# Score, bias and last-expert products on all 128 rows of the array, and the experts' gate cap moved behind its function

## Chip, cores and metric

The kernel runs on one core of one Trainium2 chip. The metric is the device time of one execution in microseconds (us). A profiled execution gives the trace that is quoted below; times of unprofiled runs give the median.

## What is computed

One layer of a decoder on x of 1024 tokens x 1024 channels, in float32. The reference, cut to the parts that the change touches:

```python
s = jnp.einsum('bdhnqc,bdhnkc->bdhnqk', qs, kk)      # 8 heads of 64 channels, causal, three dilated patterns
...
def expert_block(args):                               # top 4 of 32 experts per token
    tok, e = args
    xb = h_pad[tok]
    g = jnp.minimum(xb @ w_gate[e] + b_gate[e], SWIGLU_LIMIT)
    u = jnp.clip(xb @ w_up[e] + b_up[e], -SWIGLU_LIMIT, SWIGLU_LIMIT)
    act = (u + 1.0) * (g * jax.nn.sigmoid(SWIGLU_ALPHA * g))
    return act @ w_down[e] + b_down[e]
```

SWIGLU_LIMIT is 7, SWIGLU_ALPHA 1.702. Ahead of the experts stand an input projection, a gated unit along chunks of 128 tokens, the attention, an output projection with a layer norm, and the router; behind them a last layer norm.

## The kernel before

**Precision.** TensorE (PE) multiplies float32 operands that were split in two: a rounded part in the format fp32r (`h`) and the rest (`l`). A product of two splits takes three matmuls, high x high, low x high and high x low (`mm3`, L122 to L125).

**Front (to about 575 us).** Tokens and weights are loaded and split, and four head groups g = 0 to 3 go through the steps that the string `FRONT` names: V (values and the gated unit's input), K and Q (keys and queries), A (attention), U and S (the gated unit). The program is written in that order, but a scheduler orders the instructions of each engine, so projections of the next group stand between the attention's steps. Then the output projection (`mix`), the layer norm and the router follow for eight tiles of 128 tokens.

The attention of one group handles two heads, 64 channels each. `queries` puts each head's rounded queries on rows 0 to 63 and once more on rows 64 to 127 (`qh[h]`); the rest of both heads shares one tile `ql`, each on its own 64 rows. `keys` puts the rounded keys of a head on its own 64 rows of `ks[h]` and their rest on the other 64. So one product over 128 rows gives qh x (kh + kl), and a second one over the head's own 64 rows adds ql x kh:

```python
TE.matmul(ps[:, :w], qh[h][:, t], ks[h][:, b:b + w], start=True, stop=False)    # L371
TE.matmul(ps[:, :w], ql[c, t], ks[h][c, b:b + w], start=False, stop=True)       # L372, c: 64 rows
```

The width w is at least 256. DVE adds the mask table and takes the minimum (L373), ACT exponentiates (L376), DVE scales (L378), PE transposes (L384), ACT or DVE copies (L388, L386), and PE multiplies by the values (L393, 64 columns of the array). Working tiles named `t2` (three buffers) serve the two tanh chains and the gated unit.

**Experts (about 600 to 1970 us).** 32 experts are sorted by load into slots; `CAPS` gives each slot's room: 16 wide ones (136 to 256 tokens), 15 narrow ones of 128 and a last one of 64. A wide expert and a narrow one alternate. For each expert 12 weight pieces of 1 MB come in through SP's queue (`load`, L772) into five `raw` buffers, ACT rounds a piece to fp32r (L119), DVE makes the rest in bf16 (L120), and up to four split pieces are held. In a wide expert the weights stand still in the array (`weights_still`, L821) and tokens stream; biases are added per partition from a table `bias` (L858). In a narrow one the tokens stand still (`tokens_still`, L812) and weights stream 512 columns wide; the biases come in as a first product of a one-hot tile `oh` with the bias rows `bhl`, both on 64 rows (L835). The last expert, of 64 tokens, puts high and low tokens side by side in 128 columns, and its low products on 64 columns.

The activation stands in `gu_chain` (narrow, L695) and `gate_up_wide` (L843 on): DVE caps the gate at 7 (L698, L862), ACT applies the function (L699, L863), DVE clips up to -7..7 (L700, L867), and one DVE instruction computes (up + 1) x gate (L701, L868). The instructions on SP are kept in the order in which they are written; those of the other engines are ordered by the scheduler. The loop for left-over tokens behind the experts runs zero times or more, by data.

Of the kernel before, what the change touches and what calls it, by code (L numbers as in the profile page):

```python
# [10 lines left out]
FT = mybir.dt.float32  # L11
# [11 lines left out]
D = 1024  # L23
P = 128
# [9 lines left out]
LIMIT = 7.0  # L34
GELU_C = math.sqrt(2.0 / math.pi)
# [41 lines left out]
def layer(tc, i, out):  # L77
# [22 lines left out]
    perm = cp.tile([64, E], FT, name="perm")  # L100
# [211 lines left out]
    def sgu(g):  # L312
        vn, u, (ws, bs) = vn_of.pop(g), u_of.pop(g), ws_of.pop(g)
        at = big("t4", 3)
        for half in range(2):
            ps = bank("mm", (P, 4, P))
            for n in range(4):
                for h in range(2):
                    TE.matmul(ps[h * 64:h * 64 + 64, n], vn[:, half * 4 + n, h * 64:h * 64 + 64],
                              ws[:, h, :], start=True, stop=True)  # L320
            t = A.tile([P, 512], FT, name="t2", bufs=3)
            V.tensor_tensor(t.rearrange("p (n c) -> p n c", c=P), ps,
                            bs.to_broadcast([P, 4, P]), op=OP.add)
            d = slice(half * 512, half * 512 + 512)
            V.scalar_tensor_tensor(at[:, d], u[:, d], 0.5, t, op0=OP.mult, op1=OP.mult)
        store(0, g, at)

    q_of, k_of = {}, {}

    def queries(g, proj):  # L330
        qh = [big(f"qh{h}", 1, FR) for h in range(2)]
        ql = big("ql", 1, FR)
# [9 lines left out]
        q_of[g] = qh, ql  # L342

    def keys(g, proj):
        ks = [big(f"ks{h}", 1, FR) for h in range(2)]
        for half in range(2):
            ps = proj(half)
            s = slice(half * 512, half * 512 + 512)
            for h in range(2):
# [4 lines left out]
        k_of[g] = ks  # L354

    def attend(g):
        (qh, ql), ks, va = q_of[g], k_of[g], va_of[g]
        bt = big("t4", 3)
        for qt in range(NT):
            n = (qt + 1) * P  # L360
            pts = []
            for h in range(2):
                c = slice(h * 64, h * 64 + 64)
# [3 lines left out]
                for b in range(0, n, 512):  # L367
# [4 lines left out]
                    TE.matmul(ps[:, :w], ql[c, t], ks[h][c, b:b + w], start=False, stop=True)  # L372
# [88 lines left out]
    zero = A.tile([P, 512], FT, name="t2", bufs=3)  # L461
# [47 lines left out]
    bd = A.tile([3 * E, D], FR, name="ql")  # L509
# [31 lines left out]
    def rank():  # L541
# [10 lines left out]
        V.tensor_scalar(perm, ie[:64], kc[:, 1:2], None, op0=OP.is_equal)  # L552
# [4 lines left out]
    def logits(t, x, sums):  # L557
# [17 lines left out]
        else:  # L575
            V.tensor_scalar(mu[:, 1:2], mu[:, 0:1], 1.0 / 32, None, op0=OP.mult)
            sq = A.tile([P, 2], FT, name="sq", bufs=2)
            for q in range(2):
                junk = A.tile([P, 512], FT, name="t2", bufs=3)
# [115 lines left out]
    def gu_chain(pool, gp, up, n, tag, dst, inside=False):  # L695
        g = gp if inside else pool.tile([P, 512], FT, name=tag, bufs=3)
        u = up if inside else pool.tile([P, 512], FT, name=tag, bufs=3)
        V.tensor_scalar(g[:n], gp, LIMIT, None, op0=OP.min)  # L698
        S.activation(g[:n], g[:n], AF.Gelu_apprx_sigmoid)  # L699
        V.tensor_scalar(u[:n], up, -LIMIT, LIMIT, op0=OP.max, op1=OP.min)  # L700
        V.scalar_tensor_tensor(dst[:n], u[:n], 1.0, g[:n], op0=OP.add, op1=OP.mult)  # L701

    with (tc.tile_pool(name="c", bufs=1, reuse_waits="tile") as C,
          tc.tile_pool(name="cpsum", bufs=1, space=PSUM, reuse_waits="tile") as CP):
        left = C.tile([64, P], FT, name="left")
        V.memset(left, 0.0)
        V.memset(left[:, 0:64], 1.0)
        onesr = C.tile([64, P], FT, name="onesr")
# [15 lines left out]
        def fetch(r):  # L724
# [30 lines left out]
        def prepare(b):  # L755
# [3 lines left out]
            b.Xb = C.tile([P, KT, n], BF, name="xb" + size)  # L759
# [5 lines left out]
            if not b.wide:  # L765
                b.oh = C.tile([64, P], FR, name="oh", bufs=2)
# [36 lines left out]
        def tokens_still(p, n, x, xb, h, l, kq, first):  # L803
# [41 lines left out]
        def gate_up_wide(b, half, between):  # L845

            n, v = b.n, []
            for m in range(2):
# [12 lines left out]
                if m == 0:  # L861
                    V.tensor_scalar(t, t, LIMIT, None, op0=OP.min)  # L862
# [4 lines left out]
            V.tensor_scalar(u, u, -LIMIT, LIMIT, op0=OP.max, op1=OP.min)  # L867
            V.scalar_tensor_tensor(u, u, 1.0, g, op0=OP.add, op1=OP.mult)  # L868
# [5 lines left out]
        def room(b):  # L874
# [4 lines left out]
            b.Ab = C.tile([P, KT, b.n], BF, name="ab" + size)  # L879

        def turn(b, half):
            if not b.wide:
                c, n = slice(half * 4, half * 4 + 4), b.n
                turned(b.A[:, c, 0:n], b.A[:, c, n:2 * n], b.Ab[:, c],
# [42 lines left out]
        bhl = C.tile([64, 2, D], FR, name="bhl")  # L927

        def narrow_biases():
            for n in range(2):  # L930
# [3 lines left out]
                S.activation(bhl[:, n], br, AF.Copy)  # L934
# [34 lines left out]
    with tc.For_i(0, more, 1) as j:  # L969
        with tc.tile_pool(name="o", bufs=1) as O, tc.tile_pool(name="op", bufs=1, space=PSUM) as OPS:  # L970
# [37 lines left out]
            for half in range(2):  # L1008
                d = slice(half * 512, half * 512 + 512)
                v = []  # L1010
                for m in range(2):
                    ps = times(xs, e, [half * 4 + m, half * 4 + 2 + m])
                    t = O.tile([P, 512], FT, name="gu", bufs=2)
                    V.tensor_tensor(t, ps, bias[:, m, d], op=OP.add)
# [96 lines left out]
```

## Time and profile before

| what | value |
| --- | --- |
| median of 3 runs | 2012.61 us (2011.72 to 2015.56) |
| the profiled execution | 2018.92 us |
| its span, first to last instruction | 2017.1 us |
| mean granted clock of TensorE | 0.973 of full speed |
| DMA, mean over the span | 246 GB/s |

How to read it: busy times of engines overlap, so they don't add up to the span. PE is TensorE's matmuls, PEld its weight loads, DVE the vector engine, ACT the scalar engine, POOL GpSimd, SP the queue that issues most transfers. A row names the line, the engine, the operation and the tiles it writes and reads. For PE the row also has the part of the array that is used: 128\*128 is the full array, 64\*128 half of its rows, 128\*64 half of its columns. The clock has two levels, 1.2 and 2.4 GHz, and the mean of a stretch says how long each was granted.

### The profile page before, as it was taken

How to read it: one execution, taken by the hardware profiler on the slowest of the kernel's cores; microseconds unless marked ns; L12 is line 12 of the kernel's file. 1: busy time of each engine (PE TensorE's matmuls, PEld its weight loads, DVE VectorE, ACT ScalarE, POOL GpSimd, SP SyncE). 2: the span in 40 equal slices, each digit the busy share in tenths (PEclk: the TensorE clock that was granted, in tenths of full speed). 3: DMA queues.
4: the chain of work that ended last, by engine and by line, in shares of the span. 5: the costliest groups of instructions: out<-in, count | busy, mean ns of one | idle time of the engine just before them, and what ended most of it. 6: DMA issues, size and time to landing. Idle time of an engine off the chain costs nothing.

```text
span 2017.1 us, 32818 instructions
## 1 busy us (share of the span) xinstructions
PE 1915.5 (95%) x12423; PEld 1560.2 (77%) x12484; DVE 1582.4 (78%) x2233; ACT 1332.9 (66%) x1761; POOL 306.4 (15%) x197
## 2 busy tenths in 40 slices
PE   7999999999949999999999999999999999999991
PEld 6787686678837888788888888888888888888861
DVE  4644745577759798788888888888988988988895
ACT  4443434563337787687778778778877887887873
POOL 2112110042320112021101102011111110101110
PEclk9999999989969999999999999999999999999996
DMA  5111010162258898799889889988989989998874
GB/s 188 45 47 45 24 39 11 37 202 80 90 207 298 277 366 296 277 322 367 296 285 360 302 314 324 359 322 300 364 308 316 363 306 335 329 344 335 307 271 174
DMA packets 92657, 495.94 MB, mean 246 GB/s; under 512 B 20264, under 2 KB 20824, under 8 KB 43344
## 3 DMA queue, kind: packets, MB, share of 16 engines
q1 hardware_dynamic: 76128, 442.49, 59.6%
q0 software_dynamic: 14064, 42.92, 8.7%
q10 hardware_dynamic: 2304, 8.39, 1.1%
q8 instruction: 100, 1.64, 0.3%
q14 instruction: 61, 0.50, 0.1%
HBM read 457.04 MB, written 36.72 MB: 245 GB/s over the span
## 4 chain that ended last, share of the span: by engine, by line
PE 61%; DVE 4%; DMA 3%; ACT 2%; issue 1%; POOL 0%; SPq 0%; POOLq 0%; ACTq 0%; DVEq 0%
PE b L821 32%; PE b L812 24%; PE b L751 2%; DVE wl L120 2%; ACT wh L119 2%; PE b L920 1%; PE b L835 1%; DMA raw<-in_w_moe 1%; DMA ys<-o,tg 1%; DVE y L1056 1%; DVE y L1055 0%; DMA table<-pay,dst 0%; POOL table L626 0%; DMA y<-ys 0%; DMA xg<-hs,tg 0%
## 5 line engine op out<-in xcount | busy, mean ns | idle before, releaser
L120 DVE TENSOR_TENSOR wl<-raw,wh 128x2048 bf16<-128x2048 f32 (+1 forms) x385 | 877.0, 2283 | 135.9 <-ACT wh L119 130.7
L119 ACT ACTIVATE wh<-raw 128x2048 fp32r<-128x2048 f32 (+1 forms) x394 | 742.9, 1894 | 149.9 <-PE b L812 41.1
L821 PE MATMUL b<-xw,wh 128*128 128x272 f32 (+12 forms) x2048 | 353.4, 326 | 0.0
L821 PEld LDWEIGHTS b<-xw,wh 128*128 128x128 f32 x2048 | 319.8, 189 | 12.4
L812 PE MATMUL b<-wh,xt 128*128 128x512 f32 x992 | 271.0, 414 | 0.0
L821 PEld LDWEIGHTS <-wl 128*128 128x128 bf16 x3072 | 225.7, 98 | 15.1 <-issue 5.6
L812 PEld LDWEIGHTS b<-wh,xt 128*128 128x128 f32 x992 | 181.3, 188 | 59.7 <-issue 15.7
L742 POOL DMA_INDIRECT xg<-hs,tg x48 | 73.7, 1536 | 838.4 <-PE b L751 391.2
L821 PE MATMUL b<-aw,wh 128*128 128x272 f32 (+12 forms) x1024 | 174.3, 325 | 0.0
L923 POOL DMA_INDIRECT ys<-o,tg x48 | 113.5, 2364 | 376.8 <-ACT o L921 156.4
L821 PE MATMUL b<-xbw,wl 128*128 128x136 bf16 (+12 forms) x2048 | 165.9, 239 | 0.0
L821 PEld LDWEIGHTS b<-aw,wh 128*128 128x128 f32 x1024 | 159.6, 188 | 6.1
L856 ACT ACTIVATE sb<-b 128x136 f32<-128x136 f32 (+12 forms) x256 | 78.3, 317 | 90.3 <-PE b L821 85.4
L812 PE MATMUL b<-wh,at 128*128 128x512 f32 x496 | 137.0, 417 | 0.0
L812 PE MATMUL b<-wl,xbt 128*128 128x512 bf16 (+1 forms) x467 | 116.0, 380 | 2.7
L812 PEld LDWEIGHTS b<-wh,at 128*128 128x128 f32 x496 | 92.5, 189 | 25.4 <-issue 2.0
L858 DVE SCALAR_TENSOR_TENSOR tw<-b,bias,sb 128x136 f32<-128x136 f32 (+12 forms) x256 | 91.6, 393 | 14.5 <-ACT sb L856 13.7
L812 PEld LDWEIGHTS <-xbt 128*128 128x128 bf16 (+1 forms) x512 | 45.3, 99 | 62.8 <-issue 17.8
L821 PE MATMUL b<-abw,wl 128*128 128x136 bf16 (+12 forms) x1024 | 83.0, 239 | 0.0
L908 ACT ACTIVATE sb<-b 128x136 f32<-128x136 f32 (+12 forms) x128 | 38.8, 314 | 60.1 <-PE b L821 51.0
L388 ACT ACTIVATE pt<-tp 128x512 f32<-128x512 f32 (+3 forms) x80 | 38.0, 498 | 59.2 <-PE tp L384 58.9
L123 PE MATMUL mm<-xh,wh 128*128 128x512 f32 x160 | 69.5, 434 | 6.5 <-DVE ks L353 6.5
(357 smaller groups left out, 2930.2 us busy)
## 6 DMA issues: line engine op xcount, KB each, us to landing
raw<-in_w_moe SPq DMA_DIRECT2D x384, 1024.0 KB, 7.0
raw<-in_w_in SPq DMA_DIRECT2D x18, 512.0 KB, 3.7
raw<-in_w_out SPq DMA_DIRECT2D x8, 512.0 KB, 3.7
t<-in_x SPq DMA_DIRECT2D x8, 512.0 KB, 3.4
hs<-pt ACTq DMA_DIRECT2D x8, 512.0 KB, 5.1
ys<-pr ACTq DMA_DIRECT2D x8, 512.0 KB, 2.6
y<-ys SPq DMA_DIRECT2D x8, 512.0 KB, 6.6
out<-y SPq DMA_DIRECT2D x8, 512.0 KB, 2.6
```

The source lines that it names most:

```text
L119: S.activation(hi, src, AF.Copy)
L120: by.tensor_tensor(lo, src, hi.bitcast(FT), op=OP.subtract)
L123: TE.matmul(o, ah, bh, start=start, stop=False)
L388: S.activation(pt[:, b:e], tp[:, :e - b], AF.Copy)
L742: k.got = G.indirect_dma_start(out=k.x[:k.n], out_offset=None, in_=hs, in_offset=bass.IndirectOffsetOnAxis(ap=k.idx, axis=0))
L751: TE.transpose(tp[:, j], src(j), ident[:n, :n])
L812: TE.matmul(o, a, b, start=first and q == 0, stop=kq == 1 and q == len(every) - 1)
L821: TE.matmul(o, a, b, start=kq == 0 and j == 0, stop=kq == 1 and j == 3)
L856: S.activation(x2[:, :n], p[f][:, n:2 * n], AF.Copy)
L858: V.scalar_tensor_tensor(t[:, f * n:f * n + n], p[f][:, :n], b.bias[:, c:c + 1], x2[:, :n], op0=OP.add, op1=OP.add)
L908: S.activation(x2[:, :n], p[:, n:2 * n], AF.Copy)
L923: G.indirect_dma_start(out=ys, out_offset=bass.IndirectOffsetOnAxis(ap=k.idx, axis=0), in_=k.o[:k.n], in_offset=None, compute_op=OP.add)
```

## The change

1. **Scores.** Each head gets a `ql[h]` of its own, in bf16, zero on the other head's 64 rows; the keys are also kept as one bf16 tile `kb` (a DVE copy out of PSUM, 8 of 128 x 512). The second score product then runs over all 128 rows, in bf16, and is only as wide as needed.
2. **Bias products.** `oh` and `bhl` get 128 rows, the upper 64 of them zero.
3. **Last expert.** `Xb` and `Ab` are padded with zeros from 64 to 128 columns, so that its low products use the full array.
4. **Gate.** The cap at 7 moves behind the function: min(f(x), TOP) with TOP = f(7), inside the final DVE instruction. ACT reads the gate's sum directly. The "+ 1" of up goes into its bias (for wide experts one DVE instruction of 128 x 8 per expert behind the bias transfer, for narrow ones once), and the clip becomes -6..8.
5. `t2` has two buffers instead of three; the tile `bd` takes the room of `ssq1` instead of `ql`.

The diff, cut to what is spoken of:

```diff
+TOP = LIMIT / (1.0 + math.exp(-1.702 * LIMIT))
...
-        s = A.tile(shape, FT, name="t2", bufs=3)
+        s = A.tile(shape, FT, name="t2", bufs=2)
...
+    ql = [big(f"ql{h}", 1, BF) for h in range(2)]
+    for h in range(2):
+        G.memset(ql[h][64 - h * 64:128 - h * 64], 0.0)
...
-                V.scalar_tensor_tensor(ql[c, s], ps[c], -0.125, qh[h][c, s].bitcast(FT),
+                V.scalar_tensor_tensor(ql[h][c, s], ps[c], -0.125, qh[h][c, s].bitcast(FT),
...
+        kb = big("kb", 1, BF)
         for half in range(2):
             ps = proj(half)
             s = slice(half * 512, half * 512 + 512)
+            V.tensor_copy(kb[:, s], ps)
...
                     TE.matmul(ps[:, :w], qh[h][:, t], ks[h][:, b:b + w], start=True, stop=False)
-                    TE.matmul(ps[:, :w], ql[c, t], ks[h][c, b:b + w], start=False, stop=True)
+                    TE.matmul(ps[:, :e - b], ql[h][:, t], kb[:, b:e], start=False, stop=True)
...
-        V.tensor_scalar(g[:n], gp, LIMIT, None, op0=OP.min)
-        S.activation(g[:n], g[:n], AF.Gelu_apprx_sigmoid)
-        V.tensor_scalar(u[:n], up, -LIMIT, LIMIT, op0=OP.max, op1=OP.min)
-        V.scalar_tensor_tensor(dst[:n], u[:n], 1.0, g[:n], op0=OP.add, op1=OP.mult)
+        S.activation(g[:n], gp, AF.Gelu_apprx_sigmoid)
+        V.tensor_scalar(u[:n], up, 1.0 - LIMIT, 1.0 + LIMIT, op0=OP.max, op1=OP.min)
+        V.scalar_tensor_tensor(dst[:n], g[:n], TOP, u[:n], op0=OP.min, op1=OP.mult)
...
+                V.tensor_scalar(b.bias[:, 8:], b.bias[:, 8:], 1.0, None, op0=OP.add)
...
-            b.Xb = C.tile([P, KT, n], BF, name="xb" + size)
+            b.Xb = C.tile([P, KT, max(n, P)], BF, name="xb" + size)
+            if n <= 64:
+                G.memset(b.Xb[:, :, n:], 0.0)
...
-                b.oh = C.tile([64, P], FR, name="oh", bufs=2)
+                b.oh = C.tile([P, P], FR, name="oh", bufs=2)
...
-            rows = [slice(0, n), slice(n, 2 * n)] if n > 64 else [slice(0, 64 + n)]
-            high = [(p[:n] if n > 64 else p[:64 + n], x[:, k, r], h[:, k % 4]) for k in ks for r in rows]
-            low = [(p[:n], xb[:, k], l[:, k % 4]) for k in ks]
+            rows = [slice(0, P), slice(P, 2 * n)][:n // 64]
+            high = [(p, x[:, k, r], h[:, k % 4]) for k in ks for r in rows]
+            low = [(p, xb[:, k], l[:, k % 4]) for k in ks]
...
-                    V.tensor_scalar(t, t, LIMIT, None, op0=OP.min)
...
-            V.tensor_scalar(u, u, -LIMIT, LIMIT, op0=OP.max, op1=OP.min)
-            V.scalar_tensor_tensor(u, u, 1.0, g, op0=OP.add, op1=OP.mult)
+            V.tensor_scalar(u, u, 1.0 - LIMIT, 1.0 + LIMIT, op0=OP.max, op1=OP.min)
+            V.scalar_tensor_tensor(u, g, TOP, u, op0=OP.min, op1=OP.mult)
...
-            b.Ab = C.tile([P, KT, b.n], BF, name="ab" + size)
+            b.Ab = C.tile([P, KT, max(b.n, P)], BF, name="ab" + size)
+            if b.n <= 64:
+                G.memset(b.Ab[:, :, b.n:], 0.0)
...
-        bhl = C.tile([64, 2, D], FR, name="bhl")
+        bhl = C.tile([P, 2, D], FR, name="bhl")
+        G.memset(bhl[64:].bitcast(FT), 0.0)
...
-                S.activation(bhl[:, n], br, AF.Copy)
+                if n:
+                    V.tensor_scalar(br, br, 1.0, None, op0=OP.add)
+                S.activation(bhl[:64, n], br, AF.Copy)
```

**How the order moves.** The rows below are those of the built programs, in the order in which an engine takes them; a row stands for equal instructions that follow each other. First PE near the end of the last group's attention, before (L371 and L372 the two score products, L384 transposes, L393 the product with the values, L123 to L125 a projection of the gated unit):

```order
L393 MATMUL po<-pt,va 64x128 x11
L371 MATMUL s<-ks_3225,qh_3125 128x512
L372 MATMUL s<-ks_3225,ql 128x512
L371 MATMUL s<-ks_3225,qh_3125 128x512
L372 MATMUL s<-ks_3225,ql 128x512
L371 MATMUL s<-ks_3226,qh_3126 128x512
L372 MATMUL s<-ks_3226,ql 128x512
L125 MATMUL mm<-xh_130,wl 128x512
```

and of the change (line numbers are higher by five: L376 and L377 are the score products, L389 transposes, L398 the values):

```order
L126 MATMUL mm<-xh_142,wl 128x512
L398 MATMUL po<-pt,va 64x128 x11
L376 MATMUL s<-ks_3234,qh_3135 128x512
L377 LDWEIGHTS ql_174
L377 MATMUL s<-kb,ql_174 128x512
L376 MATMUL s<-ks_3235,qh_3136 128x512
L389 MATMUL tp<-ident,pr 128x128 x7
L377 LDWEIGHTS ql_175
L377 MATMUL s<-kb,ql_175 128x512
L124 MATMUL mm<-xh_148,wh 128x512
L125 MATMUL mm<-xl_149,wh 128x512
```

The second score product now has a weight load in a row of its own and reads `kb` and one head's `ql`. Two of the projection's products that stood between the scores stand elsewhere; the scheduler has ordered this whole stage anew.

DVE, in the second half of a narrow expert, before (L120 splits weights and tokens, L698 caps the gate, L700 clips up, L701 multiplies):

```order
L120 TENSOR_TENSOR wl<-raw,wh 128x2048
L698 TENSOR_SCALAR t<-b 128x512
L120 TENSOR_TENSOR wl<-raw,wh 128x2048
L767 TENSOR_SCALAR oh<-onesr,perm 64x128
L120 TENSOR_TENSOR at<-b,at 128x4x128
L120 TENSOR_TENSOR wl<-raw,wh 128x2048
L700 TENSOR_SCALAR t<-b 128x512
L120 TENSOR_TENSOR wl<-raw,wh 128x2048
L701 SCALAR_TENSOR_TENSOR act<-t 128x512
L120 TENSOR_TENSOR wl<-raw,wh 128x2048
```

and of the change (L121, L706 and L707 are the split, the clip and the product):

```order
L121 TENSOR_TENSOR wl<-raw,wh 128x2048 x2
L776 TENSOR_SCALAR oh<-onesr,perm 128x128
L121 TENSOR_TENSOR at<-b,at 128x4x128
L121 TENSOR_TENSOR wl<-raw,wh 128x2048
L706 TENSOR_SCALAR t<-b 128x512
L707 SCALAR_TENSOR_TENSOR act<-t 128x512
L121 TENSOR_TENSOR wl<-raw,wh 128x2048 x2
```

The cap is gone from DVE, and a weight split stands behind the product instead of between clip and product.

DVE, between the two halves of the wide expert of 240 tokens, before (L858 adds the bias):

```order
L120 TENSOR_TENSOR wl<-raw,wh 128x2048
L120 TENSOR_TENSOR at<-b,at 128x4x128
L120 TENSOR_TENSOR aw<-tw,aw 128x4x240
L120 TENSOR_TENSOR wl<-raw,wh 128x2048 x2
L120 TENSOR_TENSOR xt<-b,xt 128x4x128 x2
L120 TENSOR_TENSOR wl<-raw,wh 128x2048 x3
L858 SCALAR_TENSOR_TENSOR tw<-b,bias,sb 128x240 x4
```

and of the change (L741 is the new "+ 1" on the next wide expert's bias, L867 the adding of the bias):

```order
L876 SCALAR_TENSOR_TENSOR tw<-tw 128x960
L121 TENSOR_TENSOR wl<-raw,wh 128x2048
L121 TENSOR_TENSOR at<-b,at 128x4x128
L121 TENSOR_TENSOR aw<-tw,aw 128x4x240
L121 TENSOR_TENSOR wl<-raw,wh 128x2048 x2
L121 TENSOR_TENSOR xt<-b,xt 128x4x128 x2
L121 TENSOR_TENSOR wl<-raw,wh 128x2048
L741 TENSOR_SCALAR bias<-bias 128x8
```

The "+ 1" stands behind one weight split that follows the token splits, and two weight splits stand behind it. On SP's queue the bias transfer stands where it stood.

## Rows read from the trace of the kernel before

**Rows 1.** The page, part 1: busy us, share of the span, instructions.

```profile
PE 1915.5 (95%) x12423; PEld 1560.2 (77%) x12484; DVE 1582.4 (78%) x2233; ACT 1332.9 (66%) x1761; POOL 306.4 (15%) x197
```

**Rows 2.** Busy us: sum of four attention stretches, and the expert stage.

```profile
core 0: us, PE busy (x) PEld busy (x) DVE busy (x) ACT busy (x) POOL busy (x), PEclk, DMA share, GB/s
...
sum 254.00, PE 251.41 PEld 174.84 DVE 165.31 ACT 132.73 POOL 39.90; mean PE 62.85 PEld 43.71 DVE 41.33 ACT 33.18 POOL 9.97
...
600.00:1950.00 1350.00, 1343.95 (x9054) 1116.98 (x9113) 1175.30 (x1137) 1055.20 (x1228) 175.40 (x90) 1.00 0.91 323
```

**Rows 3.** Timeline of PE, a narrow expert: start us, us, engine, line, operation, tiles.

```profile
644.33 0.49 PE L835 MATMUL b<-bhl,oh 64*128 64x512 f32 x1
644.75 2.13 PE L812 MATMUL b<-wh,xt 128*128 128x512 f32 x8
646.72 1.90 PE L812 MATMUL b<-wl,xbt 128*128 128x512 bf16 x8
648.27 1.05 PE L812 MATMUL b<-wh,xt 128*128 128x512 f32 x3
```

**Rows 4.** Timeline of PE, attention of the last group, 409 us.

```profile
409.20 0.51 PE L371 MATMUL s<-ks,qh 128*128 128x512 f32 x1
409.63 0.49 PE L372 MATMUL s<-ks,ql 64*128 64x512 f32 x1
410.05 0.50 PE L371 MATMUL s<-ks,qh 128*128 128x512 f32 x1
```

**Rows 5.** The same, 402 us: a score pair between projections.

```profile
402.33 0.40 PE L371 MATMUL s<-ks,qh 128*128 128x512 f32 x1
402.65 0.50 PE L372 MATMUL s<-ks,ql 64*128 64x512 f32 x1
403.08 0.50 PE L123 MATMUL mm<-xh,wh 128*128 128x512 f32 x1
```

**Rows 6.** Timeline of the weight loads (PEld), the same place.

```profile
402.09 0.19 PEld L371 LDWEIGHTS s<-ks,qh 128*128 128x128 f32 x1
402.65 0.18 PEld L372 LDWEIGHTS s<-ks,ql 64*128 64x128 f32 x1 [0.37 <-issue]
```

**Rows 7.** All instructions of L372 and L835: count, duration ns min/median/max, forms.

```profile
L372 PE MATMUL s<-ks,ql x96: 378/465/502, 59.8 to 415.6; 64*128 64x512 f32 x48, 64*128 64x256 f32 x32, 64*128 64x384 f32 x16
...
L835 PE MATMUL b<-bhl,oh x64: 471/498/503, 638.1 to 1952.5; 64*128 64x512 f32 x64
```

**Rows 8.** Groups of the page, part 5: busy us, mean ns of one, idle before.

```profile
L821 PEld LDWEIGHTS <-wl 128*128 128x128 bf16 x3072 | 225.7, 98 | 15.1 <-issue 5.6
```

**Rows 9.** Groups of DVE over the span: the gate caps.

```profile
L698 DVE TENSOR_SCALAR t<-b 128x512 f32<-128x512 f32 x30 | 20.4, 681 | 0.0
...
L862 DVE TENSOR_SCALAR tw<-tw 128x544 f32<-128x544 f32 (+12 forms) x32 | 16.6, 520 | 0.4
```

**Rows 10.** Waits of PE, 45 to 430 us: total us, times, longest.

```profile
PE mm L123 <- DVE ks L353: 6.5, 3, 3.0
```

**Rows 11.** Timeline of PE, last expert.

```profile
1962.70 0.43 PE L751 MATMUL b<-ident,act 64*128 64x64 f32 x4 [1.56 <-DVE act L701]
...
1965.56 1.92 PE L812 MATMUL b<-wl,abt 128*64 128x512 bf16 x4 [2.43 <-ACT abt L753]
```

**Rows 12.** Short stretches, columns as in rows 2.

```profile
60.00:68.00 8.00, 8.00 (x24) 4.99 (x23) 6.01 (x17) 4.41 (x12) 4.71 (x2) 0.79 0.32 81
156.00:164.00 8.00, 5.00 (x13) 3.68 (x12) 4.52 (x6) 2.96 (x5) 1.10 (x2) 0.66 0.15 22
308.00:312.00 4.00, 4.00 (x12) 2.79 (x11) 2.82 (x9) 0.94 (x3) 0.58 (x1) 0.60 0.42 131
```

**Rows 13.** Timeline of SP and DVE, 797 us; landing times of L734.

```profile
796.95 0.33 SPq L734 DMA_DIRECT2D bias<-in_b_guT  x1
...
798.43 2.29 DVE L120 TENSOR_TENSOR wl<-raw,wh 128x2048 bf16<-128x2048 f32 x1
...
DMA to landing us min/median/max: 3.5/4.0/6.3
```

More of the change, by code (lines that the diff above doesn't have):

```diff
@@ L99, in layer @@
     cnt = cp.tile([64, E], FT, name="cnt")
-    perm = cp.tile([64, E], FT, name="perm")
+    perm = cp.tile([P, E], FT, name="perm")
     order = cp.tile([1, E], I32, name="order")
@@ L320, in sgu @@
                               ws[:, h, :], start=True, stop=True)
-            t = A.tile([P, 512], FT, name="t2", bufs=3)
+            t = A.tile([P, 512], FT, name="t2", bufs=2)
             V.tensor_tensor(t.rearrange("p (n c) -> p n c", c=P), ps,
@@ L339, in queries @@
                     S.activation(qh[h][o * 64:o * 64 + 64, s], ps[c], AF.Copy, scale=-0.125)
-                V.scalar_tensor_tensor(ql[c, s], ps[c], -0.125, qh[h][c, s].bitcast(FT),
+                V.scalar_tensor_tensor(ql[h][c, s], ps[c], -0.125, qh[h][c, s].bitcast(FT),
                                        op0=OP.mult, op1=OP.subtract)
-        q_of[g] = qh, ql
+        q_of[g] = qh
     def keys(g, proj):
         ks = [big(f"ks{h}", 1, FR) for h in range(2)]
+        kb = big("kb", 1, BF)
         for half in range(2):
@@ L353, in keys @@
                 V.tensor_tensor(ks[h][o, s], ps[c], ks[h][c, s].bitcast(FT), op=OP.subtract)
-        k_of[g] = ks
+        k_of[g] = ks, kb
     def attend(g):
-        (qh, ql), ks, va = q_of[g], k_of[g], va_of[g]
+        qh, (ks, kb), va = q_of[g], k_of[g], va_of[g]
         bt = big("t4", 3)
@@ L362, in attend @@
             for h in range(2):
-                c = slice(h * 64, h * 64 + 64)
                 t = slice(qt * P, qt * P + P)
@@ L458, in layer @@
             output_weights()
-    zero = A.tile([P, 512], FT, name="t2", bufs=3)
+    zero = A.tile([P, 512], FT, name="t2", bufs=2)
     V.memset(zero, 0.0)
@@ L508, in layer @@
         G.dma_start(out=br[q * E:q * E + E], in_=i["b_down"])
-    bd = A.tile([3 * E, D], FR, name="ql")
+    bd = A.tile([3 * E, D], FR, name="ssq1")
     S.activation(bd, br, AF.Copy)
@@ L551, in rank @@
         V.tensor_scalar(jk, key, kc[:, 0:1], None, op0=OP.is_gt, op1=OP.add, accum_out=kc[:, 1:2])
-        V.tensor_scalar(perm, ie[:64], kc[:, 1:2], None, op0=OP.is_equal)
+        V.memset(perm[64:], 0.0)
+        V.tensor_scalar(perm[:64], ie[:64], kc[:, 1:2], None, op0=OP.is_equal)
         po = bank("mm", (P, E))
@@ L578, in logits @@
             for q in range(2):
-                junk = A.tile([P, 512], FT, name="t2", bufs=3)
+                junk = A.tile([P, 512], FT, name="t2", bufs=2)
                 S.activation(junk, x[:, q * 512:q * 512 + 512], AF.Square, scale=1.0 / 32, bias=mu[:, 1:2],
@@ L697, in gu_chain @@
         u = up if inside else pool.tile([P, 512], FT, name=tag, bufs=3)
-        V.tensor_scalar(g[:n], gp, LIMIT, None, op0=OP.min)
-        S.activation(g[:n], g[:n], AF.Gelu_apprx_sigmoid)
-        V.tensor_scalar(u[:n], up, -LIMIT, LIMIT, op0=OP.max, op1=OP.min)
-        V.scalar_tensor_tensor(dst[:n], u[:n], 1.0, g[:n], op0=OP.add, op1=OP.mult)
+        S.activation(g[:n], gp, AF.Gelu_apprx_sigmoid)
+        V.tensor_scalar(u[:n], up, 1.0 - LIMIT, 1.0 + LIMIT, op0=OP.max, op1=OP.min)
+        V.scalar_tensor_tensor(dst[:n], g[:n], TOP, u[:n], op0=OP.min, op1=OP.mult)
     with (tc.tile_pool(name="c", bufs=1, reuse_waits="tile") as C,
           tc.tile_pool(name="cpsum", bufs=1, space=PSUM, reuse_waits="tile") as CP):
-        left = C.tile([64, P], FT, name="left")
+        left = C.tile([P, P], FT, name="left")
         V.memset(left, 0.0)
         V.memset(left[:, 0:64], 1.0)
-        onesr = C.tile([64, P], FT, name="onesr")
+        onesr = C.tile([P, P], FT, name="onesr")
         V.memset(onesr, 1.0)
@@ L883, in turn @@
                 c, n = slice(half * 4, half * 4 + 4), b.n
-                turned(b.A[:, c, 0:n], b.A[:, c, n:2 * n], b.Ab[:, c],
+                turned(b.A[:, c, 0:n], b.A[:, c, n:2 * n], b.Ab[:, c, :n],
                        lambda j: b.act[half][:n, j * P:j * P + P], n)
@@ L1013, in layer @@
                     t = O.tile([P, 512], FT, name="gu", bufs=2)
-                    V.tensor_tensor(t, ps, bias[:, m, d], op=OP.add)
+                    V.scalar_tensor_tensor(t, ps, float(m), bias[:, m, d], op0=OP.add, op1=OP.add)
                     v.append(t)
```

1 line of the change is left out of this document (removed).

## Prediction

> **What bounds the kernel now.** I read the busy shares first, then engine times by stage, then single products of TensorE in the stages that the change touches. The shares say that PE is busy 95% of the span, DVE 78% and ACT 66% [rows 1]. By stage it is sharper. In the four stretches that hold the attention of one head group each, 254 us, PE is busy 251.4 us and DVE 165.3, which is 65%; in the expert stage, 600 to 1950 us, PE is busy 1344 of 1350 us and DVE 1175 [rows 2]. So PE is the bound in both. But a busy PE in this profile is not a PE at its pace, because the modelled ends of products overlap. The pace is read from start to start.
>
> On the full array, eight products of 512 fp32 columns and eight of 512 bf16 columns take 648.27 - 644.75 = 3.52 us, 0.22 each [rows 3]. In the attention, where a full-array product (L371, 128\*128) alternates with one on half the rows (L372, 64\*128), the starts are 0.42 to 0.43 us apart, both ways [rows 4]: 0.20 us are lost each time that the tile form changes. Where one L372 stands alone between full-array products, it costs 0.32 on the way in and 0.43 on the way out [rows 5], 0.09 and 0.20 us over the pace. The weight loads show why: the load of L371 starts at 402.09, 0.24 us ahead of its own product, and so lies beside the product before it; that of L372 starts together with its product, at 402.65 [rows 5, 6]. A load of another tile form is not hidden. The bias products of the narrow experts (L835) pay the same: 0.42 us to the next start [rows 3].
>
> **The change part by part.**
>
> Scores. There are 96 of these half-array products [rows 7]. They become full-array bf16 products. I counted the changes of tile form along PE's built order by the operands' partitions: up to the last product ahead of the experts they fall from 320 to 157 (128\*64 products, L393 and L319, keep theirs). A change costs 0.09 to 0.20 us [rows 4, 5]; most L372 stand in alternation, so I take 0.18: 163 x 0.18 = 29 us. This is off PE's own time, not yet off the span. DVE does 165 us of work in stretches of 254 in all [rows 2] that would become 29 us shorter, so its share goes from 0.65 to 0.73; the chain scores, minimum, exponential, scaling, transposes has latencies that PE now outruns more often, and the scheduler has written the front's order anew. I take 80%: 23.5 us, with ends of 12 (PE waits for DVE in most steps) and 30.
>
> The bf16 type itself. A bf16 product between fp32 ones could have a price of its own. In runs of eight none is seen: the sixteen products of rows 3 contain a switch each way and keep 0.22 us. Here the type alternates at each product, which no row shows. A bf16 load takes 98 ns [rows 8], so the ends are 0 and 96 x 0.1 = 10 us. I take 0, since rows 3 are nearest.
>
> The key copy (8 of 128 x 512). The nearest row of that size out of PSUM takes 0.68 us (L698 [rows 9]), 5.4 us of DVE in all, which DVE's idle third hides, except where PE waits for this very chain: three waits of 6.5 us in total for `ks` [rows 10]. I take 1 us of loss, ends 0 and 3 x 0.68 = 2. The third `t2` buffer that is given up costs nothing: two `mm` banks already limit the chain to two tiles.
>
> Bias products. All 64 of them [rows 7] lose the change of form on the way out, 64 x 0.195 = 12.5 us. On the way in 15 keep it, because by the order a product on 32 or 64 rows stands ahead; 49 x 0.09 (the isolated case of rows 5) = 4.4. Together 17 us, ends 12 and 64 x 0.195 + 49 x 0.20 = 22. PE has only 6 us of idle in this stage [rows 2], so nothing else sets the pace, and I take 16.
>
> The last expert. Its low products are 128\*64 [rows 11] and stand between full-array ones; by the order 14 changes go, 14 x 0.20 = 2.8 us. But its second half waits for its own chain, 1.56 and 2.43 us in two places, and more behind them [rows 11], so I take 1.5, ends 0 and 2.8.
>
> The gate cap. 30 narrow ones of 0.68 us and 32 wide ones of 0.52 leave DVE [rows 9]: 37 us of 1175. PE does not wait for them now, so they count nothing on the path. They are cover: with PE 17 us shorter, DVE's share in the stage goes from 0.87 to (1175 - 37) / 1333 = 0.85 instead of up. The padding (a few memsets, the widened one-hot and zero operands) keeps the width that sets an instruction's time and is left at nothing.
>
> The clock. In two places PE falls to half clock (1.2 GHz) inside the attention while it is busy all the time: 0.79 was granted over 60 to 68 us and 0.60 over 308 to 312 [rows 12], worth 0.21 x 8 = 1.7 and 0.40 x 4 = 1.6 us. Both lie where half-array products have begun; elsewhere the clock falls after PE idled (0.66 over 156 to 164, PE busy 5 of 8 us [rows 12]). If denser products keep the clock, 3.3 us return; if a faster PE idles more often, as many are lost. I take a gain of 1.5.
>
> **Sum:** 23.5 - 1 + 16 + 1.5 + 1.5 = 41.5 us. The profiled execution took 2018.9 us (span 2017.1), so 1977.4 for it. The median of the three runs shown is 2012.6, 6.3 lower; the same gain gives **1971 us**. The ends together: 30 + 22 + 2.8 + 3.3 = 58 us at most, and 12 - 2 + 10 - 3 = 17 at least.
>
> **A rule that speaks against it.** The rows say that loads of the same full form run ahead [rows 6]. The Trainium skill, in TensorE: Matmul & The Clock Gate, Part 3, says that a weight load overlaps with products in flight only when the row groups differ; by that the two heads' half-array loads would be the ones to hide and full-array loads would not. Rows 6 show the opposite here: the full-array load starts early and the half-array one does not. By the rows the sum stands as above; by the rule it would be that of the first rival, 2012 us.
>
> **The rivals.**
> 1. *The loads stay exposed.* If what costs 0.2 us is a load that no product covers, and alternating types or zero-padded operands leave it uncovered, then each of the 96 pairs pays 0.10 + 0.19 us (a bf16 load [rows 8] and an fp32 one [rows 6]) and each bias product 2 x 0.19: 28 + 24 = 52 us, about what the changes of form cost now. The time would be 2012, no change. For it: no row alternates the types product by product. Against: 3.52 us for sixteen [rows 3]. Chance 0.05.
> 2. *The front gives it back.* PE's gain in the attention turns into waits for DVE and ACT, with new falls of the clock behind them, since the order is another. Then some 5 us are left of 23.5, the clock's gain is gone, and the total is about 5 + 16 + 1 = 22: 1991 us. For it: DVE and ACT would be closer to their limits, and PE already waited for DVE's `ks` [rows 10]. Against: in the four stretches PE shows 2.6 us of idle in all [rows 2]. Chance 0.13.
> 3. *Slower: DVE stands behind a transfer.* The new "+ 1" on up's bias (16 wide experts) sits in DVE's order right behind a weight split, and DVE takes its work in order. In the old trace that point would be at 800.7 us (the weight split from 798.43 for 2.29); the bias transfer is issued at 796.95 and takes 3.5 to 6.3 us, median 4.0 [rows 13]. So DVE would wait about 0.3 us, at worst 2.6, and the weight splits queue behind it. Up to four split pieces are held for PE meanwhile. To end slower by over 0.2%, the 41.5 us and 4 more must go: 45.5 / 16 = 2.8 us on PE at each wide expert, more than the worst landing with no cover at all; it takes transfers that land later than any shown. Then 2017 us or more. Chance 0.03.
>
> **How the numbers follow.** The forecast has 0.79, the rivals 0.13, 0.05 and 0.03. About 0.2% (4 us) is what a measurement of this kernel can tell from no change. The forecast's own ends are 2012.6 - 58 = 1955 and 2012.6 - 17 = 1996; with rival 2 inside, the range is 1955 to 1992, and it leaves out rivals 1 and 3 and the thin ends. Faster is the forecast and rival 2, 0.92; same is rival 1, 0.05; slower is rival 3, 0.03.
>
> **What would show it.** In the new profile the second score product starts 0.22 us after the first and the next one 0.22 after it; the bias product is 0.23 from its successor; the attention stretches are 4 to 7 us shorter each; the expert stage is 15 us shorter; DVE is some 35 us less busy in it. It is wrong if starts stay at 0.4 us, if PE shows more than 10 us of new idle in the front, or if weight splits wait behind the "+ 1".

## The result, and the profile after

The changed kernel takes 1989.87 us (median of four runs, 1987.55 to 1993.05); the kernel before, run beside it, 2012.21 us. The ratio is 0.9887, 95% interval 0.9869 to 0.9904: 22.3 us faster. Forecast were 41.5 us; the time lies inside the range, near its slow end. The profiled execution took 1989.86 us, its span is 1988.0. Medians below are over all executions of a run and ratios over its fast ones: one execution, of the run that keeps both caps, took 9524.57 us and is in no ratio.

Marks in the two traces, in us from the span's start (the third column is the third experiment's run, whose front is instruction for instruction that of before):

| mark | before | front of before, another run | after |
| --- | --- | --- | --- |
| first score product | 59.6 | 59.4 | 55.7 |
| last value product of the attention | 423.9 | 416.2 | 408.5 |
| first bias product of the experts | 638.1 | 631.0 | 618.7 |
| first bias product of the last expert (64 tokens) | 1923.0 | | 1894.8 |
| end of the span | 2017.1 | | 1988.0 |

The same front takes 638 or 631 us, so what the change gained up to the experts is 12 to 19 us. From the experts' first bias product to that of the last expert it is 8.8 us less, and 0.9 less behind it, where 16 and 1.5 were forecast.

Part 1 of the page after, against [rows 1]:

```profile
PE 1864.2 (94%) x12402; PEld 1549.6 (78%) x12484; DVE 1563.0 (79%) x2195; ACT 1331.1 (67%) x1761; POOL 314.3 (16%) x202
```

The windows of the attention's four stretches and of the expert stage, against [rows 2]:

```profile
core 0: us, PE busy (x) PEld busy (x) DVE busy (x) ACT busy (x) POOL busy (x), PEclk, DMA share, GB/s
56.00:118.00 62.00, 59.04 (x441) 45.25 (x445) 44.71 (x126) 32.52 (x70) 9.76 (x8) 1.00 0.16 49
180.00:240.00 60.00, 56.98 (x387) 40.86 (x391) 46.10 (x125) 32.05 (x67) 9.76 (x8) 1.00 0.17 50
289.00:341.00 52.00, 46.14 (x345) 33.00 (x348) 36.99 (x103) 31.07 (x65) 5.24 (x3) 1.00 0.10 32
353.00:409.00 56.00, 51.68 (x365) 36.60 (x368) 41.88 (x106) 35.00 (x68) 17.06 (x8) 0.97 0.33 104
590.00:1920.00 1330.00, 1316.42 (x9003) 1112.70 (x9065) 1138.56 (x1082) 1045.80 (x1221) 178.96 (x92) 1.00 0.91 325
```

In the attention PE is busy 213.8 of 230 us; it was 251.4 of 254. PE idles 16 us there instead of 2.6, and DVE's share is 169.7 / 230 = 0.74, the 0.73 of the forecast. In the expert stage PE idles 13.6 us; it was 6.

The score products, PE's timeline in the first lines of the last attention, against [rows 4, 5]:

```profile
354.93 0.28 PE L376 MATMUL s<-ks,qh 128*128 128x256 f32 x1
355.05 0.28 PE L377 MATMUL s<-kb,ql 128*128 128x256 bf16 x1
355.09 0.42 PE L376 MATMUL s<-ks,qh 128*128 128x384 f32 x1
355.35 0.34 PE L377 MATMUL s<-kb,ql 128*128 128x384 bf16 x1
355.39 0.53 PE L124 MATMUL mm<-xh,wh 128*128 128x512 f32 x1
355.76 0.39 PE L125 MATMUL mm<-xl,wh 128*128 128x512 f32 x1
355.99 0.40 PE L126 MATMUL mm<-xh,wl 128*128 128x512 f32 x1
```

Two pairs of 256 and 384 columns and one product of 512 take 355.76 - 354.93 = 0.83 us for 1792 columns, 0.46 ns a column; the pace of [rows 3] is 0.43. The 0.2 us at each change of form are gone. (The record of a bf16 product starts just ahead of the next one's, so pairs are read together. 18 of the 96 have no record.)

Waits of PE between the first score and the last value product, against three waits of 6.5 us for `ks` [rows 10] and 1.8 us of others:

```profile
PE mm L124 <- DVE ks L359: 6.9, 3, 3.6
PE tp L389 <- DVE pr L383: 4.7, 4, 1.5
PE mm L124 <- DVE t L323: 3.4, 1, 3.4
PE mm L320 <- DVE t L323: 1.7, 2, 0.9
PE s L376 <- DVE m L378: 1.6, 1, 1.6
PE s L376 <- DVE m L382: 1.2, 2, 0.6
PE tp L389 <- DVE m L382: 1.0, 1, 1.0
```

With smaller ones it is 22.6 us, where it was 8.3: PE now waits for DVE's scaling (`pr`), for its minimum and reciprocal (`m`, L378 and L382) and for the gated unit (`t`).

In the expert stage:

```profile
PE b L844 <- DVE tw L919: 6.7, 4, 2.8
PE b L830 <- DVE wl L121: 2.5, 2, 1.7
```

From one narrow expert's first bias product to the next (the last expert counts as narrow here), the spacing fell by 1.2 to 1.6 us in most of the 15 intervals, but two grew: the second from 93.9 to 98.1 us and the fourth from 90.2 to 94.2. In each, PE waits 2.7 to 2.8 us for `tw`, behind 16 transposes (L758), and then falls to half clock. The wait in the second, and both falls:

```profile
729.15 1.81 PE L758 MATMUL b<-ident,xg 128*128 128x128 f32 x16
733.74 0.50 PE L844 MATMUL b<-bhl,oh 128*128 128x512 f32 x1 [2.78 <-DVE tw L919]
734.00:738.00 4.00, 3.78 (x11) 2.52 (x12) 4.00 (x6) 2.31 (x6) 0.77 (x1) 0.57 1.00 365
915.00:919.00 4.00, 3.28 (x9) 2.61 (x9) 4.00 (x7) 1.98 (x5) 0.00 (x0) 0.57 0.98 369
```

Before, PE kept the full clock through this stage. So there are two questions: where the front's gain went, and what makes two pairs of experts long.

### The profile page after: what moved, and what is told of

The parts are those of the page before. It is cut to its first block, busy times and chain, and to the rows that moved or that the text cites. A ratio compares the mean times of both kernels' runs of the same rounds, so it can differ in the third digit from the quotient of the medians.

```text
span 1988.0 us, 32785 instructions
## 1 busy us (share of the span) xinstructions
PE 1864.2 (94%) x12402; PEld 1549.6 (78%) x12484; DVE 1563.0 (79%) x2195; ACT 1331.1 (67%) x1761; POOL 314.3 (16%) x202
## 4 chain that ended last, share of the span: by engine, by line
PE 60%; DMA 4%; DVE 4%; issue 2%; ACT 2%; POOL 0%; SPq 0%; POOLq 0%; ACTq 0%; DVEq 0%
PE b L830 32%; PE b L821 23%; DMA raw<-in_w_moe 2%; PE b L758 2%; DVE wl L121 2%; PE b L930 1%; ACT wh L120 1%; DMA ys<-o,tg 1%; PE b L844 1%; DVE y L1069 1%; DVE y L1068 0%; DMA y<-ys 0%; DMA table<-pay,dst 0%; POOL table L632 0%; DMA xg<-hs,tg 0%
## 5 line engine op out<-in xcount | busy, mean ns | idle before, releaser
L121 DVE TENSOR_TENSOR wl<-raw,wh 128x2048 bf16<-128x2048 f32 (+1 forms) x385 | 874.9, 2284 | 151.1 <-ACT wh L120 149.8
L120 ACT ACTIVATE wh<-raw 128x2048 fp32r<-128x2048 f32 (+1 forms) x394 | 742.4, 1893 | 143.8 <-PE b L821 37.9
L821 PEld LDWEIGHTS b<-wh,xt 128*128 128x128 f32 x992 | 188.5, 190 | 47.5
L749 POOL DMA_INDIRECT xg<-hs,tg x48 | 78.7, 1639 | 791.1 <-PE b L758 353.4
L821 PE MATMUL b<-wl,xbt 128*128 128x512 bf16 x465 | 116.0, 380 | 2.9 <-issue 0.2
L867 DVE SCALAR_TENSOR_TENSOR tw<-b,bias,sb 128x136 f32<-128x136 f32 (+12 forms) x256 | 91.5, 393 | 15.8 <-ACT sb L865 14.8
L821 PEld LDWEIGHTS <-xbt 128*128 128x128 bf16 x512 | 45.0, 98 | 63.2 <-issue 18.1
L124 PE MATMUL mm<-vh,xh 128*128 128x256 f32 x256 | 72.6, 284 | 0.6 <-DVE ql L344 0.6
```

The source lines that it names most:

```text
L120: S.activation(hi, src, AF.Copy)
L121: by.tensor_tensor(lo, src, hi.bitcast(FT), op=OP.subtract)
L124: TE.matmul(o, ah, bh, start=start, stop=False)
L749: k.got = G.indirect_dma_start(out=k.x[:k.n], out_offset=None, in_=hs, in_offset=bass.IndirectOffsetOnAxis(ap=k.idx, axis=0))
L821: TE.matmul(o, a, b, start=first and q == 0, stop=kq == 1 and q == len(every) - 1)
L867: V.scalar_tensor_tensor(t[:, f * n:f * n + n], p[f][:, :n], b.bias[:, c:c + 1], x2[:, :n], op0=OP.add, op1=OP.add)
```

## The experiments

### The parts alone

**Scores alone**: all edits of points 1 and 5 on the kernel before.

> The kernel before with the score part alone (full-array bf16 products, key copy, two t2 buffers). PE has 29 us less of tile-form changes in the front. Theory A (most of it is kept, the changed kernel's loss lies in the experts): 20 to 24 us faster, about 1989 to 1992. Theory B (PE's gain in the attention turns into waits for DVE, ACT and half clock): 8 to 14 us faster, and PE shows 15 us or more of waits over 0.15 us in the attention stretches, 2 us or so before. The expert stage keeps the length of before, 1350 us, under both.

1997.54 us against 2015.81, ratio 0.9914 (0.9896 to 0.9932): 17.3 us, between the two theories. The waits of PE in the attention are those of the changed kernel line by line (6.9, 4.7, 3.4, 1.7 us and on), and the expert stage is as before. So the front's gain is short by itself, and the experts' loss lies elsewhere.

**Bias products alone** (point 2).

> The kernel before with the bias part alone (one-hot and bias rows on 128 rows, the lower 64 zero-padded). Theory A (64 changes of tile form on the way out and 49 on the way in, nothing else on the path): 15 to 18 us faster, each narrow expert about 1.35 us shorter, no interval longer. Theory B (a shorter expert outruns its weights: the transfers of the stretch between two narrow experts set the pace): two pairs of experts grow by 4 to 5 us and show half clock, 8 to 11 us faster in all.

1996.50 us, ratio 0.9905 (0.9888 to 0.9921): 19.2 us. Of the 15 intervals 14 shrink by 0.5 to 1.4 us, one grows by 1.7. From the first bias product to that of the last expert it is 1269.7 us instead of 1284.9, and 1.3 less behind it: 16.5 in the trace. It is theory A by the time. The interval that grows, the eighth, holds a wait of 1.7 us and a fall of the clock behind it, with the old gate: there too two weight splits (`wl`), 4.49 us in a row, stand ahead of the DVE instructions that take a product out of PSUM (`tw`, the evictions), and PE waits for these.

**Gate alone** (point 4).

> The kernel before with the gate part alone (the cap behind the function, the 1 in up's bias). DVE has 35 us less in the expert stage. Theory A (it was cover, not path): within 2 us of before. Theory B (the two long pairs of experts in the changed kernel come from here, by the addition behind the bias transfer or by another order of the splits): about 5 to 10 us slower, with two pairs of experts 4 to 5 us longer. Theory C (DVE's relief frees weight splits earlier): 3 us or more faster.

2020.89 us, ratio 1.0031 (1.0020 to 1.0042): 6.2 us **slower**. It is theory B by the time, with one long pair and not two: the fourth interval is 94.8 us instead of 90.2, with a fall of the clock, the second and the sixth are 1.1 and 1.6 longer. PE's waits for `tw` in the stage, before and with the gate alone:

```profile
PE b L835 <- DVE tw L909: 1.4, 4, 0.6
PE b L837 <- DVE tw L910: 5.1, 3, 2.8
```

The gate costs in the last expert too. With the narrow gate new, PE waits 4.0 to 5.0 us there for DVE's `act`, in all five traces that have it; with the old one it is 1.6 to 2.6 in the other nine. From that expert's first bias product to the end it is 96.1 us here and 94.1 before.

**Everything but the gate**: the changed kernel with point 4 undone.

> The changed kernel with the gate part undone, so scores, bias and last expert together. Theory A (the gate part is cover that the shorter PE time needs): slower than the changed kernel, 1992 or more. Theory B (the gate part brings the late weights): 5 to 10 us faster than the changed kernel, 1980 to 1985, and the two long pairs are gone. If the parts only add up, the gain is the sum of the first two runs' gains and 1 to 2 us for the last expert.

1981.60 us, ratio 0.9834 (0.9818 to 0.9850): 33.5 us faster than before, and by the two ratios 0.5%, some 10 us, faster than the changed kernel. The second interval is 92.6 us (98.1), the fourth 90.6 (94.2). The parts add up: 17.3 + 19.2 against 33.5, within the intervals. What hurts is the gate.

### What in the gate costs time

**The old cap kept beside the new one.**

```diff
+        V.tensor_scalar(g[:n], gp, LIMIT, None, op0=OP.min)
-        S.activation(g[:n], gp, AF.Gelu_apprx_sigmoid)
+        S.activation(g[:n], g[:n], AF.Gelu_apprx_sigmoid)
...
+                    V.tensor_scalar(t, t, LIMIT, None, op0=OP.min)
                     S.activation(t, t, AF.Gelu_apprx_sigmoid)
```

> The changed kernel with the old cap instruction put back ahead of the function, beside the new one, and the 1 still in up's bias: DVE has its 35 us again, and ACT's built order behind the first expert is that of the fourth run. Theory A (the loss comes from the order that the scheduler writes once the cap is gone: the gate's function moves ahead of weight roundings on ACT): 1981 to 1983, as the fourth run, and no pair of experts is long. Theory B (it comes from the addition behind the bias transfer): as the changed kernel, 1988 to 1991, with the two long pairs.

1979.21 us, ratio 0.9827 (0.9813 to 0.9842): theory A. More work on DVE, the same "+ 1" behind the bias transfer, and the 10 us are back. So neither the addition nor DVE's load is the cause. In the expert stage PE's and ACT's traces have the order of the run before this one, and DVE's has it but for the additions; in the changed kernel DVE's and ACT's orders differ from it in many places. So it is what the missing instruction does to the order. With it goes a second difference that was not tried alone: without the cap, in narrow experts ACT, and not DVE, reads the gate's sum out of PSUM. But no wait of PE in the stage of the changed kernel is for that; the long ones are for DVE's `tw`. DVE's timeline in the second interval, in the changed kernel:

```profile
725.97 0.70 DVE L919 TENSOR_TENSOR tw<-b,sb 128x136 f32<-128x136 f32 x3
726.59 2.28 DVE L121 TENSOR_TENSOR wl<-raw,wh 128x2048 bf16<-128x2048 f32 x1
728.79 0.29 DVE L919 TENSOR_TENSOR tw<-b,sb 128x136 f32<-128x136 f32 x1
729.00 4.48 DVE L121 TENSOR_TENSOR wl<-raw,wh 128x2048 bf16<-128x2048 f32 x2
733.40 0.94 DVE L919 TENSOR_TENSOR tw<-b,sb 128x136 f32<-128x136 f32 x4
734.26 2.28 DVE L121 TENSOR_TENSOR wl<-raw,wh 128x2048 bf16<-128x2048 f32 x1
736.46 2.34 DVE L121 TENSOR_TENSOR xw<-b,xw 128x512 fp32r<-128x512 f32 x4
739.50 2.29 DVE L121 TENSOR_TENSOR wl<-raw,wh 128x2048 bf16<-128x2048 f32 x1 [0.70 <-ACT wh L120]
```

and with the old cap kept:

```profile
723.43 2.29 DVE L121 TENSOR_TENSOR wl<-raw,wh 128x2048 bf16<-128x2048 f32 x1
725.63 0.71 DVE L921 TENSOR_TENSOR tw<-b,sb 128x136 f32<-128x136 f32 x3
726.25 2.29 DVE L121 TENSOR_TENSOR wl<-raw,wh 128x2048 bf16<-128x2048 f32 x1
728.45 0.30 DVE L921 TENSOR_TENSOR tw<-b,sb 128x136 f32<-128x136 f32 x1
728.66 2.29 DVE L121 TENSOR_TENSOR wl<-raw,wh 128x2048 bf16<-128x2048 f32 x1
730.86 0.71 DVE L921 TENSOR_TENSOR tw<-b,sb 128x136 f32<-128x136 f32 x3
731.48 2.29 DVE L121 TENSOR_TENSOR wl<-raw,wh 128x2048 bf16<-128x2048 f32 x1
733.68 0.30 DVE L921 TENSOR_TENSOR tw<-b,sb 128x136 f32<-128x136 f32 x1
```

With the cap, one weight split stands between two groups of evictions. Without it, two splits stand there, 4.48 us, and the bias product that needs a bank waits 2.8 us for `tw`. PE stands, and the clock falls. Two splits ahead of such evictions are nothing new: the old order has them in every interval but the second, fourth and sixth, and in its trace PE waits 0.2 us for `tw` there at most. That DVE's order makes the loss and not ACT's, which moved with it, is read from the trace at these places; the two were not tried apart.

**Only the narrow experts' gate new**, and **only the wide ones'**.

> The changed kernel with the wide experts' gate undone, the narrow ones' kept new. Theory A1 (the narrow gate function, moved ahead on ACT, delays a weight rounding): 1987 to 1991, long pairs as in the changed kernel. Theory A2 (the wide one's order does it): 1980 to 1983. In a mixture each of this run and the next is 3 to 5 us over 1981.6.

> The changed kernel with the narrow experts' gate undone, the wide ones' kept new, with the addition behind the bias transfer. Theory A1 (the narrow gate brings the loss): 1980 to 1983. Theory A2 (the wide gate brings it): 1987 to 1991.

1982.87 us, ratio 0.9850 (0.9833 to 0.9867), and 1981.90 us, 0.9841 (0.9826 to 0.9856). Each is 1 to 5 us slower than the two runs that keep the old cap everywhere (0.9834 and 0.9827), within the intervals, where the two together lose 10. The parts of this loss do not add: each order has one longer interval (the fourth, 92.0 us, in the first; the sixth, 91.0, in the second) and one fall of the clock; the changed kernel has two, longer ones. Nor is the wait the same: in the first run PE waits 2.1 us for a weight rounding on ACT (`wh`), as theory A1 had it, in the second 2.3 us for `tw`.

**The gate new from the seventh expert on** (`if ORDER.index(b.r) < 6:` ahead of the old cap).

> The changed kernel with the old cap instruction put back in the first six experts alone; from the seventh on the gate is new. The order theory puts the loss in the first four long intervals between narrow experts, where the transfers run at their limit. Then: 1978 to 1981, as with the cap everywhere, and in the later intervals 0 to 1 us less than there. If the loss moves on to the next pairs, where the new order begins: 1983 to 1988.

1985.41 us, ratio 0.9851 (0.9827 to 0.9874), runs from 1979.64 to 1989.53. The second interval is as with the cap (92.6 us). The third, where the new order begins, is 84.5 us, 0.8 over the changed kernel's. The fourth is 93.3, with a wait of 2.8 us for `tw` and a fall of the clock, as in the changed kernel (94.2). So the cap takes the loss away where it stands, and the next long pair keeps it; the interval of the time does not tell this run from those with the cap.

**Six `raw` buffers in the changed kernel.**

```diff
-RAWS = 5
+RAWS = 6
...
-        g = gp if inside else pool.tile([P, 512], FT, name=tag, bufs=3)
+        g = gp if inside else pool.tile([P, 512], FT, name=tag, bufs=2)
```

(and the same two buffers in the other two places of that tile, which makes the room.)

> The changed kernel with six raw buffers instead of five (and two t tiles instead of three, for the room). ACT's built order stays word for word, DVE's but for one row in each pair of experts, so evictions still stand behind two weight splits. Theory A (the weights that land late start the loss: the first link is ACT's wait of 3.3 and 2.8 us for a transfer, and one more buffer in flight ends it): 1976 to 1984, and the two long pairs lose 4 us or more each. Theory B (DVE's order alone makes the loss, whenever weights land): 1987 to 1992, with the two long pairs as they were. If two t tiles make the narrow activation wait: slower than the changed kernel.

1975.55 us, ratio 0.9817 (0.9801 to 0.9834): 36.9 us faster than before, 14 faster than the changed kernel, the fastest of all. Theory A. The second and fourth interval are 92.6 and 88.6 us, and no clock falls there. ACT's waits in the second interval, changed kernel:

```profile
ACT wh L120 <- DMA raw<-in_w_moe: 6.9, 4, 3.3
```

With six buffers there is no such wait in that interval, though ACT's order in the stage is the same and DVE's differs only in where the additions stand. DVE's order still has the two splits in a row, but earlier, when nothing is short:

```profile
723.62 4.49 DVE L121 TENSOR_TENSOR wl<-raw,wh 128x2048 bf16<-128x2048 f32 x2
728.02 0.71 DVE L919 TENSOR_TENSOR tw<-b,sb 128x136 f32<-128x136 f32 x3
```

and this is all of PE's waits from 590 to 1900 us:

```profile
PE b L844 <- DVE tw L919: 0.3, 1, 0.3
```

So in these two pairs the loss needs both: weights that land late (there are such waits with the cap too, 5.8 us), and an order that puts evictions behind two splits. The sixth interval of the run with the wide gate alone fits less well: PE waits 2.3 us there, and ACT 1.9 us for transfers. Six buffers with the old cap were not tried. The longer wait in the last expert stays with six buffers (4.8 us).

### Where the front's gain went

**Key copy on POOL**, out of the rounded keys (base: everything but the gate).

```diff
-            V.tensor_copy(kb[:, s], ps)
...
                 S.activation(ks[h][c, s], ps[c], AF.Copy)
+                G.tensor_copy(kb[c, s], ks[h][c, s].bitcast(FT))
```

> The fourth run's kernel (no gate part) with the bf16 key copy made by POOL from the rounded keys in SBUF, instead of by DVE out of PSUM; the values are the same to bf16. Theory A (the key copy on DVE stands in the chain to ks and is 3 to 6 us of the front's loss): 1976 to 1979. Theory B (the front's loss lies in the attention's own chain of DVE and ACT): 1980 to 1983. If POOL is slow with 8 of 64 x 512 per group, or shares DVE's port, slower: 1983 to 1990.

1978.12 us, ratio 0.9833 (0.9817 to 0.9849), against 0.9834 without the edit: no difference, within some 5 us. The trace says the same more sharply: PE's waits for `ks` are 6.7 us with the copy on POOL, 6.9 with it on DVE, and were 6.5. The key copy is not the loss.

**Two `t2` buffers alone**, on the kernel before.

> The kernel before with two t2 buffers instead of three, nothing else. Theory A (the third buffer is worth nothing, and the front's loss in the first run has another cause): within 3 us of before. Theory B (the buffer that was given up makes the tanh chains and the gated unit late, and part of the front's loss is this): 4 to 8 us slower, with new waits of PE for DVE in the front.

2014.53 us, ratio 1.0000 (0.9988 to 1.0011). Theory A.

**No second score product** (base: everything but the gate; the output lacks low queries x keys).

> The fourth run's kernel without the second score product at all, so the scores leave out low queries x keys (96 bf16 products fewer, about 16 us of PE at 0.22 us for 512 columns with the shorter ones counted by width). Theory A (PE still sets the front's pace, and the 29 us that were saved are on the path): 13 to 18 us faster than the fourth run in the front. Theory B (the chain of scores, minimum, exponential, scaling and transposes, on DVE and ACT, sets the pace in most steps): 8 us or less.

1965.26 us, ratio 0.9757 (0.9737 to 0.9778). The experts begin at 600.8 us instead of 617.6: 16.8 us for 36,864 columns, which are 15.8 us at the 0.22 us for 512 of [rows 3]. By the two ratios it is 15.5 us, 10 to 21. Theory A: PE's own work still sets the front's pace, and a price of the bf16 products beyond their columns can't be told (the front of the trace with them also was at half clock for some 7 us more). The waits do not shrink with less work on PE:

```profile
PE tp L387 <- DVE pr L381: 11.1, 9, 1.9
PE mm L123 <- DVE ks L358: 6.9, 3, 3.6
```

In the first three groups nearly all sit at fixed places (the head of each attention, the keys), not in each step; in the last group PE now waits for `pr` at five places, up to 1.5 us.

## Why the prediction was right in kind and long in size

**Scores: the mechanism holds, the share was too high.** Taken from all starts between the first score and the last value product (each interval less the product's own pace, waits and half of the time at half clock), changes of form cost 54.6 us in the run with the front of before and 22.1 after: 32.5 gone, 29 forecast. The share kept failed: "I take 80%: 23.5 us". The scores alone gave 17.3 us (13.7 to 21.0), and 3.7 of it are none of this, but the earlier first score (below). So some 13.6 us of 29, under half. The rest went into waits: PE's named ones rose from 8.3 to 22.6 us, by 14.3. The clock is not it: the run with the scores alone was granted 0.976 in the mean of its executions, the kernel before beside it 0.975. The forecast named this loss ("latencies that PE now outruns more often") and had its lower end at 12; the idle of 10 us that it set as a sign against itself came. That the rewritten order places these waits fits their fixed places, but it was not tried. The attention stretches themselves, 356.9 and 352.8 us, differ by only 4 us, and can't be held against each other as they stand: the second holds 48 products that stood behind it before, and 5.1 us lost to half clock where the first had none. With bf16 records missing too, a few us stay unassigned.

**Key copy, `t2`, type.** 1 us, 0 and 0 were taken; the runs show no loss for any of the three, within some 5 us for the first and the last and some 2 for `t2`.

**The start, not forecast.** The first score comes 3.7 us earlier in the mean: at 54.8 to 56.3 us in the ten traces with the score part, at 58.3 to 59.8 in the four without. In the order of before, DVE's multiply `ws` stands ahead of token and weight splits and waits for its transfer:

```profile
DVE ws L306 <- DMA ws<-in_sgu_wT: 5.7, 1, 5.7
```

In the new order a split goes ahead of it, and 1.8 us are left:

```profile
DVE ws L307 <- DMA ws<-in_sgu_wT: 1.8, 1, 1.8
```

PE's wait for the first `wl` fell from 4.3 us to 0.6. That is luck of the order; the prediction compared orders only at the attention. Without it the gain would be some 18.6 us and the time 1993.6, outside the range.

**Bias products: right.** 16 taken, 16.5 in the trace and 19.2 (15.9 to 22.6) by the times. The successor's start is 0.32 us behind (median; 0.43 before), not 0.23:

```profile
624.68 0.50 PE L844 MATMUL b<-bhl,oh 128*128 128x512 f32 x1
625.01 2.04 PE L821 MATMUL b<-wh,xt 128*128 128x512 f32 x8
```

but a narrow expert with its four is 1.3 us shorter in an undisturbed interval, 0.32 each. The working has a slip here that changes nothing: its lower end is 12, and the sum of the ends takes 10.

**Last expert.** 1.5 taken. From the last expert's first bias product to the end it is 92.8 us with the bias part alone and 91.8 with the last expert added: 1 us, in single traces. With the gate it is 93.2: PE's longer wait for `act` took more than that.

**Gate: the step that failed most.** "PE does not wait for them now, so they count nothing on the path." DVE did lose its instructions and did stay under PE; but removing 37 us of work nobody waited for cost 6 us alone and 10 in company. The step read DVE's share and not the order that the scheduler writes, in which a split of 2.28 us ahead of an eviction of 0.2 decides when PE gets its bank.

**The clock.** A gain of 1.5 us was taken. The two falls in the attention of [rows 12] went, others came, two of them in the expert stage: no gain, and the mean granted clock is 0.972 in the changed kernel's executions, 0.975 in those of the kernel before beside the scores alone. Nor do half-array products explain the old falls: in the run with the gate alone, whose front has the same products in the same order, the clock is full from 23 to 425 us.

**The rivals.** The time is that of the second rival, 1991, by another way: it left 5 us of the front and all of the bias, and 17 and 16 to 19 were left, less the gate's 10. Against the first rival stands the pace above, and in the new trace the load of a full-array product still runs ahead, by 0.23 us for the L125 product at 355.76, shown with the result:

```profile
355.53 0.19 PEld L125 LDWEIGHTS mm<-xl,wh 128*128 128x128 f32 x1
```

The Trainium skill (TensorE: Matmul & The Clock Gate, Part 3) says that a weight load overlaps with products in flight only when the row groups differ. This trace does not agree: that load and the product before it use all rows, and the changes of form that went took 32.5 us with them. The third rival's place is harmless: DVE waits 1.9 us in all for the bias transfers, longest 0.8, and both caps with that addition ran in 1979.

## What to carry to other kernels

Before counting a removed instruction as free, compare the order that the scheduler writes without it, on the engines that release PSUM banks: two long splits ahead of a short eviction can cost more than the instruction did. Where a stage runs with transfers at their limit, try one more buffer in flight too; here it took back what the gate had cost between the experts. Of time taken off the bound engine in a stage whose second engine is at 0.65 of it, this case kept about half, not four fifths.

## Not expected of the hardware

A removal made the kernel slower, in twelve runs, through order: 6.2 us. Bf16 products on the full array between fp32 ones cost about their columns (15.5 us, 10 to 21, for 96 of them; 15.8 by their width). And PE fell to half clock after waits of 1.7 to 2.8 us in a stage where it is busy 99% of the time; the fall in the second interval (0.57 granted over 4 us, 1.7 us) adds more than half of the wait's 2.8 us again.
